# A two-layer hybrid decoder: two plain groups instead of three at the feed-forward's entry, parameters on SyncE's queue, first weights in halves, last outputs scaled by ScalarE and sent on two queues

## Chip, cores and metric

The kernel runs on one core of a Trainium2 chip. The metric is the device time of one execution in microseconds, lower is better. Times of before and after are medians of several runs; the profile shows one execution of its own.

## What is computed

Two layers on 1024 tokens of width 1024, in float32. Cut to what matters here:

```python
for l in range(DEPTH):                                   # DEPTH = 2
    h = rmsnorm(x, attn_norm[l])
    proj = h @ w_in[l]                                   # split among four mixers
    ...                                                  # attention, gated conv, pooling, windowed attention
    mixed = per_group_rmsnorm(...) * mix_norm[l]
    x = x + mixed @ w_o[l]
    h2 = rmsnorm(x, ffn_norm[l])
    gate, up = jnp.split(h2 @ w_gate_up[l], 2, axis=-1)  # D_FF = 2816 = 22 x 128
    x = x + (jax.nn.silu(gate) * up) @ w_down[l]
return rmsnorm(x, final_norm)
```

## The kernel before

**Layout.** Activations lie transposed, channels on the 128 partitions, tokens along the row in two halves of 512 (`HT`). The 1024 channels are 8 tiles (`NK`), the 2816 inner channels of the feed-forward 22 (`NFF`).

**Matmuls.** Every float32 operand is split into two parts that TensorE multiplies at its fast float32 rate: `hi`, rounded by a copy on ScalarE, and `lo`, the rest, by a subtraction on VectorE (`split`, L283 and L284; with a gain per channel L286 and L287). A product of a 128x128 block with 128x512 activations is then three matmuls (`mm3`, L272): hi by hi, hi by lo, lo by hi.

**The start.** The parameters (norm gains and such, `par`) are loaded by GpSimd's queue (L131). The weights of the first three projections and the input x (`enter`, L366) come on SyncE's queue; `weights` (L203 on) loads a tile of 128x1024 with one DMA (L207), copies it to `hi` (L215) and subtracts (L216). The x tiles are scaled with the attention norm's gains from `par` while they are split, and their squares are added up on the way (L313, L318, L324) for the norm. The list of weights to come is written by `expect_layer`.

**The feed-forward's first half** makes gate and up for 22 groups of 128 inner channels. A *plain* group (`plain`, L1268) multiplies the weight blocks with the activation blocks directly: for each half of the tokens, four products of four blocks (2 for the gate, 2 for up). The other groups pair channel tiles and token halves as 2x2 blocks and need seven products in place of eight (the loop at L1466, helper `gu_start`). They use sums of the weight blocks, made by GpSimd (`sums`, L1132 to L1134, `sum4`, L1154), and differences of the activation blocks, made by VectorE from the residual (`combine`, L1054: per pair of channel tiles the differences N1, N2, T3, T4, L1063 to L1071, each of which is then split in two). In a seven-product group the first product takes B11, the second B21 (both split when the residual is added in `out_last`, L1099), the third N2, then N1, T3, B22 and T4. Between products ScalarE copies a partial result out of PSUM (`snap`, L1176), and VectorE adds (L1188, L1512, L1524) and multiplies with the norm (`mul_to`, L348). The silu is ScalarE's (L1311), its product with the norm GpSimd's (L1312).

Three groups are plain (`NPL = 3`, L42). They are what TensorE works on while `combine`, the norm of the residual (`norm`) and the first weight sums are made; the order in which these are written is L1426 to L1465. The two half splits of a plain group's weights are `split_plain`; a seven-product group's are `split1` to `split4`, one wide split for each of the first three and a narrow one.

Beside this GpSimd adds up blocks of the down projection's weights (`dn_sums`, L161), four additions of 256 columns at a time. The activations of each pair of groups are combined on VectorE and written to DRAM (`combos`, L1314), to be read back for the down projection, which also takes seven products.

**The end.** In the last layer the last products (B22) of the down projection are made for 256 tokens at a time (L1641 on). For each piece the result is added to the residual (`evac`, L1577), squared and summed over channels, and the norm follows: a matmul with ones (L336), three steps on ScalarE (L338 to L340), two on VectorE (L341, L344). Then `finish` (L375) multiplies each of the 8 tiles by the final norm's gain and the norm in one VectorE instruction (L380) and sends it out on SyncE's queue (L384).

**The order** in which each engine works is not that of the program's text. `steps_of` lists all instructions, `length` estimates each one's duration, and `arrange` places them on the engines one after the other, by rank and by when their inputs are ready. `MOVES` shifts the rank of some 400 numbered groups of instructions by hand-set amounts (`places`), and `order_engines` fixes the resulting order for each engine. Instructions, buffers and dependencies stay what the text says.

Of the kernel before, what the change touches and what calls it, by code (L numbers as in the profile page):

```python
# [15 lines left out]
ALU = mybir.AluOpType  # L16
# [25 lines left out]
NPL = 3  # L42
# [69 lines left out]
def trunk_kernel(ctx: ExitStack, tc: tile.TileContext, ins, out):  # L112
# [18 lines left out]
    pool.dma_start(par, ins["params"])  # L131
# [71 lines left out]
    def weights(src, n):  # L203
        if n > 2 * P:
            s = F.pair()
            raw = F.ap2(s)
            sp.dma_start(raw[:, :n], src)  # L207
# [7 lines left out]
        act.copy(hi[:, :n], raw[:, :n])  # L215
        dve.tensor_tensor(out=lo[:, :n], in0=raw[:, :n], in1=rd(hi[:, :n]), op=ALU.subtract)  # L216
# [20 lines left out]
    def expect_layer(l):  # L237
        for m in (2, 3, 0, 4, 5, 6, 1, 13, 14, 10, 11, 12, None, 7, 8, 9):
            if m is None:
                expect(rope_weights, l)  # L240
            else:
                expect(weights, ins["w_in"][l, m], 2 * HT)
# [132 lines left out]
    def finish(x, t, cols):  # L375

        for d in range(NK):
            a = F.ap(x[d][t])[:, cols]
            g = par[:, L * PC_N + d : L * PC_N + d + 1]
            dve.scalar_tensor_tensor(  # L380
                out=a, in0=a, scalar=g, in1=F.ap(ratt[t])[:, cols], op0=ALU.mult, op1=ALU.mult
            )
            o = out[d, :, t * HT : (t + 1) * HT]
            sp.dma_start(o[:, cols], a)  # L384

    last_silu = None
    for l in range(L):
# [1038 lines left out]
        std.append(GateUp(2))  # L1426
# [9 lines left out]
        plain_gates()  # L1436
        combine(2)
        plain_acts()
        std[2].split_plain()
        w = GateUp(3)  # L1440
# [3 lines left out]
        w.sums()  # L1444
        combine(3)
        plain_acts()
        w.split1()
        plain(2, 0)
        plain_silus()
        plain_gates()  # L1450
        w.split2()
        plain_acts()
        wn = GateUp(4)
        plain(2, 1)
        plain_silus()
# [185 lines left out]
        for cols in (slice(0, 256), slice(256, HT)) if last else ():  # L1641
            for m, p, w in tail:
# [26 lines left out]
class Step:  # L1669
    __slots__ = ("ins", "eng", "rank", "before", "after", "tiles", "left", "ns", "tail", "ready", "sums", "bank", "onchip", "size", "start", "end", "table", "rows", "place")  # L1670

    def __init__(self, eng, rank):
# [4 lines left out]
        self.onchip = False  # L1677
# [64 lines left out]
def steps_of(tc):  # L1742
    steps, seen = [], {}
    table, runs = None, {"Silu": [], "Exp": []}
    for i in tc.nc.cur_bb.bb.instructions:
# [23 lines left out]
        elif kind == "InstDMACopy":  # L1769
# [47 lines left out]
def arrange(steps, rank=lambda v: v.rank):  # L1817
# [35 lines left out]
    while any(now.values()) or any(later.values()):  # L1853
# [57 lines left out]
        else:  # L1911
# [5 lines left out]
            if e == "DVE" and v.onchip:  # L1917
                ns += 0.8 * sum(max(0.0, min(b, t + ns) - max(a, t)) for a, b in pool_busy[-8:])
# [234 lines left out]
```

## Time and profile before

| | us |
|---|---|
| median of 3 runs | 2063.41 (2063.31 to 2064.40) |
| the profiled execution | 2062.8 |
| its span, first to last instruction | 2061.0 |
| TensorE busy | 2038.0 (99%), 9442 matmuls |
| VectorE busy | 1539.8 (75%) |
| ScalarE busy | 971.0 (47%) |
| GpSimd busy | 571.3 (28%) |
| granted TensorE clock, mean | 0.998 |

In the lines below PE is TensorE, PEld its weight loads, DVE VectorE, ACT ScalarE, POOL GpSimd, SP SyncE. A line of the timeline has the start in us, the length in us, engine, line, operation, the tiles written and read, their shapes and the count of instructions run together; in brackets the idle time ahead of it and what ended it. A line of the groups has the count, then busy us and mean ns of one, then the idle time ahead. A line of the waits has who waited for whom, the sum in us, how often, the longest. A line of a stretch has each engine's busy us and its count of instructions, the clock, the share of the DMA engines and GB/s.

### The profile page before, as it was taken

What the parts mean: (1) busy time and instruction counts of PE and PEld (TensorE: products, weight loads), DVE (VectorE), ACT (ScalarE), POOL (GpSimd) and SP (SyncE); (2) the same over time, 40 slices, a digit from 0 to 9 for tenths busy, and PEclk for the clock granted to TensorE, in tenths of its full rate; (3) what the DMA queues carried; (4) which work ended last, traced back from release to release, by engine and by line L of the source; (5) the groups of instructions that cost most, each with busy time, mean ns of one, the idle gap of its engine ahead of it and who ended that gap; (6) DMA issues with size and microseconds to landing.
All of it is one profiled execution on the core that took longest, in us unless ns stands there. A gap on an engine that the chain in (4) does not pass through costs nothing.

```text
span 2061.0 us, 26301 instructions
## 1 busy us (share of the span) xinstructions
PE 2038.0 (99%) x9442; PEld 1680.9 (82%) x9442; DVE 1539.8 (75%) x2420; ACT 971.0 (47%) x1712; POOL 571.3 (28%) x453
## 2 busy tenths in 40 slices
PE   8999999999999999999999999999999999999997
PEld 6887888887888888888888878888888888888887
DVE  7888988976766767655656898878877677786555
ACT  7547556643333334444434576656433333354332
POOL 0000000047776775100000000000677677650000
PEclk9999999999999999999999999999999999999999
DMA  5110222324444446966411102233344444498652
GB/s 181 42 45 30 74 86 98 133 103 159 168 159 152 166 158 231 340 236 208 138 36 44 57 16 86 75 118 113 133 169 158 155 163 157 143 325 303 201 177 87
DMA packets 148819, 289.76 MB, mean 141 GB/s; under 512 B 12608, under 2 KB 72000, under 8 KB 148688
## 3 DMA queue, kind: packets, MB, share of 16 engines
q1 hardware_dynamic: 148656, 288.03, 40.5%
q8 instruction: 74, 1.21, 0.2%
q14 instruction: 57, 0.47, 0.1%
q0 software_dynamic: 32, 0.04, 0.0%
HBM read 204.66 MB, written 83.36 MB: 140 GB/s over the span
## 4 chain that ended last, share of the span: by engine, by line
PE 95%; DVE 2%; ACT 1%; DMA 1%; issue 1%; POOL 0%; DVEq 0%; SPq 0%; ACTq 0%; POOLq 0%
PE ps_mm L272 36%; PE ps_s L272 29%; PE ps_t L272 12%; PE ps_pv L272 8%; PE ps_pv L962 2%; PE ps_t L950 1%; PE ps_s L896 1%; PE ps_t L336 1%; PE ps_s L897 1%; PE ps_s L898 1%; PE ps_pv L572 1%; PE ps_mm L770 1%; PE ps_s L511 1%; DVE u L284 1%; PE ps_t L560 1%
## 5 line engine op out<-in xcount | busy, mean ns | idle before, releaser
L272 PE MATMUL ps_mm<-u,u 128*128 128x512 f32 (+1 forms) x3376 | 835.5, 389 | 1.4 <-DVE u L1001 1.2
L272 PEld LDWEIGHTS ps_mm<-u,u 128*128 128x128 f32 x3376 | 621.7, 188 | 126.6 <-issue 4.0
L272 PE MATMUL ps_s<-u,u 128*128 128x512 f32 x2672 | 636.0, 390 | 9.5 <-ACT u L286 7.4
L272 PEld LDWEIGHTS ps_s<-u,u 128*128 128x128 f32 x2672 | 501.6, 188 | 116.2 <-ACT u L286 7.4
L284 DVE TENSOR_TENSOR u<-u,u 128x1024 fp32r<-128x1024 f32 (+2 forms) x380 | 449.5, 1206 | 154.1 <-ACT u L283 118.9
L283 ACT CAST u<-u 128x1024 fp32r<-128x1024 f32 (+2 forms) x380 | 328.1, 888 | 480.4 <-PE ps_mm L272 192.8
L272 PE MATMUL ps_t<-u,u 128*128 128x512 f32 (+1 forms) x1212 | 284.1, 378 | 0.0
L272 PEld LDWEIGHTS ps_t<-u,u 128*128 128x128 f32 x1212 | 222.7, 188 | 43.0 <-issue 0.5
L959 POOL MEMSET u<- 128x128 f32 x32 | 5.9, 212 | 844.8 <-PE ps_mm L272 653.0
L1312 POOL TENSOR_TENSOR tp<-tp,u 128x512 f32<-128x512 f32 x88 | 144.1, 1639 | 231.6 <-ACT tp L1311 231.3
L161 POOL TENSOR_TENSOR u<-u 128x256 f32<-128x256 f32 x176 | 188.7, 1072 | 66.4 <-DVE u L284 30.5
L272 PE MATMUL ps_pv<-u,u 128*128 128x512 f32 x696 | 167.4, 389 | 0.4 <-ACT u L283 0.4
L272 PEld LDWEIGHTS ps_pv<-u,u 128*128 128x128 f32 x696 | 130.5, 188 | 28.1 <-ACT u L283 0.8
L1311 ACT ACTIVATE tp<-tp 128x512 f32<-128x512 f32 x88 | 55.5, 632 | 127.4 <-DVE tp L348 126.7
L1132 POOL TENSOR_TENSOR u<-u,u 128x512 f32<-128x512 f32 x38 | 66.9, 1761 | 140.9 <-ACT tp L1311 83.9
L286 ACT ACTIVATE u<-u,par 128x512 fp32r<-128x512 f32 x100 | 69.9, 717 | 58.0 <-DVE u L1577 18.6
L283 ACT CAST u<-ps_t 128x512 fp32r<-128x512 f32 (+4 forms) x136 | 65.1, 506 | 56.4 <-PE ps_t L950 32.5
L284 DVE TENSOR_TENSOR u<-ps_t,u 128x512 fp32r<-128x512 f32 (+4 forms) x136 | 76.9, 582 | 18.4 <-ACT u L283 17.6
L287 DVE SCALAR_TENSOR_TENSOR u<-u,par,u 128x512 fp32r<-128x512 f32 x100 | 72.7, 745 | 7.7 <-ACT u L286 7.5
L1524 DVE TENSOR_TENSOR tp<-ps_mm,tn 128x512 f32<-128x512 f32 x38 | 26.3, 691 | 61.5 <-PE ps_mm L272 61.5
L348 DVE TENSOR_TENSOR tp<-tp,u 128x512 f32<-128x512 f32 x76 | 69.0, 908 | 1.1
L318 ACT ACTIVATE tn<-u 128x512 f32<-128x512 f32 (+1 forms) x93 | 52.8, 589 | 31.8 <-DVE u L1577 28.4
(191 smaller groups left out, 2218.9 us busy)
## 6 DMA issues: line engine op xcount, KB each, us to landing
u<-in_w_gu SPq DMA_DIRECT2D x88, 512.0 KB, 4.3
ad<-u SPq DMA_DIRECT2D x154, 256.0 KB, 2.4
u<-ad SPq DMA_DIRECT2D x70, 512.0 KB, 5.4
u<-in_w_dn SPq DMA_DIRECT2D x68, 512.0 KB, 4.0
qd<-u SPq DMA_DIRECT2D x44, 512.0 KB, 2.9
u<-qd SPq DMA_DIRECT2D x32, 512.0 KB, 4.8
u<-in_w_in SPq DMA_DIRECT2D x30, 512.0 KB, 3.5
u<-in_xT SPq DMA_DIRECT2D x32, 256.0 KB, 5.1
```

Of the source, the lines that this page charges most:

```text
L161: pool.tensor_tensor(out=o, in0=o, in1=u, op=ALU.add)
L272: pe.matmul(o, w, r, start=start and k == 0 and i == 0, stop=stop and k == n - 1 and i == 2, skip_group_check=again,)
L283: act.copy(hi, f)
L284: dve.tensor_tensor(out=lo, in0=f, in1=rd(hi), op=ALU.subtract)
L286: act.activation(hi, f, AF.Copy, scale=gain)
L287: dve.scalar_tensor_tensor(out=lo, in0=f, scalar=gain, in1=rd(hi), op0=ALU.mult, op1=ALU.subtract)
L318: act.activation(q, f, AF.Square)
L348: dve.tensor_tensor(out=o, in0=a, in1=b, op=ALU.mult)
L962: pe.matmul(py[:, c0:], v_of(j, h), R.ap(s)[:, c0:], start=j == 0 and n == 0, stop=j == nj - 1 and n == 1,)
L1132: pool.tensor_tensor(out=F.ap(q + 1), in0=a21, in1=a22, op=ALU.add)
L1311: last_silu = act.activation(g, g, AF.Silu)
L1312: pool.tensor_tensor(out=g, in0=g, in1=r, op=ALU.mult)
```

## The change

- `NPL` is 2: two plain groups, the third becomes a seven-product group. The sequence at the entry is rewritten for it; `w.sums()` and `w.split1()` of the first seven-product group come earlier in the text.
- `par` is loaded by SyncE's queue.
- The weights of the very first projection are loaded, copied and subtracted in two halves of 512 columns.
- In the last piece of the end, ScalarE multiplies each output tile by its gain (`gain`) once the tile's square is taken; `finish` then multiplies by the norm alone, and the DMAs of even tiles are issued by ScalarE, of odd ones by SyncE.
- Three of the planner's estimates are changed (a GpSimd operation, VectorE next to GpSimd, a DMA issued by ScalarE), and the table `MOVES` is replaced by another.

```diff
-NPL = 3
+NPL = 2
...
-    pool.dma_start(par, ins["params"])
+    sp.dma_start(par, ins["params"])
...
-    def weights(src, n):
+    def weights(src, n, parts=1):
+        cuts = [slice(i * n // parts, (i + 1) * n // parts) for i in range(parts)]
         if n > 2 * P:
             s = F.pair()
             raw = F.ap2(s)
-            sp.dma_start(raw[:, :n], src)
+            for c in cuts:
+                sp.dma_start(raw[:, c], src[:, c])
...
-        act.copy(hi[:, :n], raw[:, :n])
-        dve.tensor_tensor(out=lo[:, :n], in0=raw[:, :n], in1=rd(hi[:, :n]), op=ALU.subtract)
+        for c in cuts:
+            act.copy(hi[:, c], raw[:, c])
+            dve.tensor_tensor(out=lo[:, c], in0=raw[:, c], in1=rd(hi[:, c]), op=ALU.subtract)
...
-                expect(weights, ins["w_in"][l, m], 2 * HT)
+                expect(weights, ins["w_in"][l, m], 2 * HT, 2 if (l, m) == (0, 2) else 1)
...
+    def gain(x, d, t, cols):
+        a = F.ap(x[d][t])[:, cols]
+        act.activation(a, a, AF.Copy, scale=par[:, L * PC_N + d : L * PC_N + d + 1])
+
-    def finish(x, t, cols):
+    def finish(x, t, cols, gained=False):
         for d in range(NK):
             a = F.ap(x[d][t])[:, cols]
-            g = par[:, L * PC_N + d : L * PC_N + d + 1]
-            dve.scalar_tensor_tensor(
-                out=a, in0=a, scalar=g, in1=F.ap(ratt[t])[:, cols], op0=ALU.mult, op1=ALU.mult
-            )
+            if gained:
+                mul_to(a, a, F.ap(ratt[t])[:, cols])
+            else:
...
-            sp.dma_start(o[:, cols], a)
+            (act if gained and d % 2 == 0 else sp).dma_start(o[:, cols], a)
...
-        std.append(GateUp(2))
+        w = GateUp(2)
         plain(0, 0)
         combine(0)
         plain(1, 0)
...
         plain_gates()
+        w.sums()
         combine(2)
         plain_acts()
-        std[2].split_plain()
-        w = GateUp(3)
+        w.split1()
         plain(1, 1)
         plain_silus()
         plain_gates()
-        w.sums()
         combine(3)
-        plain_acts()
-        w.split1()
-        plain(2, 0)
-        plain_silus()
-        plain_gates()
         w.split2()
         plain_acts()
-        wn = GateUp(4)
-        plain(2, 1)
-        plain_silus()
-        plain_gates()
...
+        wn = GateUp(3)
         w.split3()
-        plain_acts()
         plain_silus()
...
                 evac(B22, m, p, cols)
                 ss.add(1, F.ap(x[2 * m][1])[:, cols], cols)
+                for d in (2 * m, 2 * m + 1):
+                    gain(x, d, 1, cols)
             ratt[1] = ss.rnorm(1, cols, tag="s")
-            finish(x, 1, cols)
+            finish(x, 1, cols, True)
...
-        return 206 if kind == "InstMemset" else 230 + 2.07 * n
+        return 206 if kind == "InstMemset" else 1150 + 0.5 * n
...
+            elif eng == "ACT":
+                v.ns, v.tail = 450, 2400
...
-            v.onchip = not any(a.bass_ap.tensor.name.startswith("ps_") for a in ins + outs)
+            if not any(a.bass_ap.tensor.name.startswith("ps_") for a in ins + outs):
+                v.onchip = 0.7 if kind == "InstTensorScalarPtr" and len(ins) < 3 else 0.4
...
-                ns += 0.8 * sum(max(0.0, min(b, t + ns) - max(a, t)) for a, b in pool_busy[-8:])
+                ns += v.onchip * sum(max(0.0, min(b, t + ns) - max(a, t)) for a, b in pool_busy[-8:])
```

More of the change, by code (lines that the diff above doesn't have):

```diff
@@ L373, in enter_norm @@
         ratt[t] = ss.rnorm(t, parts=True)
-    def finish(x, t, cols):
+    def gain(x, d, t, cols):
+        a = F.ap(x[d][t])[:, cols]
+        act.activation(a, a, AF.Copy, scale=par[:, L * PC_N + d : L * PC_N + d + 1])
+    def finish(x, t, cols, gained=False):
         for d in range(NK):
             a = F.ap(x[d][t])[:, cols]
-            g = par[:, L * PC_N + d : L * PC_N + d + 1]
-            dve.scalar_tensor_tensor(
-                out=a, in0=a, scalar=g, in1=F.ap(ratt[t])[:, cols], op0=ALU.mult, op1=ALU.mult
-            )
+            if gained:
+                mul_to(a, a, F.ap(ratt[t])[:, cols])
+            else:
+                g = par[:, L * PC_N + d : L * PC_N + d + 1]
+                dve.scalar_tensor_tensor(
+                    out=a, in0=a, scalar=g, in1=F.ap(ratt[t])[:, cols], op0=ALU.mult, op1=ALU.mult
+                )
             o = out[d, :, t * HT : (t + 1) * HT]
-            sp.dma_start(o[:, cols], a)
+            (act if gained and d % 2 == 0 else sp).dma_start(o[:, cols], a)
     last_silu = None
@@ L1676, in __init__ @@
         self.sums = self.bank = None
-        self.onchip = False
+        self.onchip = 0.0
         self.table = self.rows = None
```

93 rows, old and new, of the table MOVES are left out of this document.

## The prediction

> **What bounds the kernel now.** I read the page's busy shares first, then what TensorE waited for, then single stretches of the timeline.
>
> ```profile
> PE 2038.0 (99%) x9442; PEld 1680.9 (82%) x9442; DVE 1539.8 (75%) x2420; ACT 971.0 (47%) x1712; POOL 571.3 (28%) x453
> PE   8999999999999999999999999999999999999997
> ```
>
> ```profile
> PE ps_s L272 <- ACT u L286: 7.4, 1, 7.4
> PE ps_s L336 <- DVE u L320: 1.4, 1, 1.4
> PE ps_mm L272 <- DVE u L1001: 1.2, 1, 1.2
> PE ps_s L272 <- DVE te L1512: 1.0, 1, 1.0
> PE ps_s L272 <- DVE tp L348: 0.5, 1, 0.5
> PE ps_s L272 <- ACT tn L1176: 0.5, 1, 0.5
> PE ps_pv L272 <- ACT u L283: 0.4, 1, 0.4
> ```
>
> TensorE works in 38 of 40 slices at nine tenths or more. What it waits for is 7.4 us ahead of its first matmul and, in these rows, 5.0 us in all behind it; L1512, L348, L1176 and the 0.4 us of L283 lie in the feed-forward's entry of layer 0 and make 2.4 us. So a microsecond of matmul work taken out is a microsecond of time, as long as nobody else is late; and little waiting is left for a better order to remove. A matmul's recorded 390 ns overlaps its neighbour, so its price comes from start to start:
>
> ```profile
> 1464.21 5.60 PE L272 MATMUL ps_s<-u,u 128*128 128x512 f32 x24
> 1469.65 5.60 PE L272 MATMUL ps_t<-u,u 128*128 128x512 f32 x24
> 1475.09 2.88 PE L272 MATMUL ps_s<-u,u 128*128 128x512 f32 x12
> ```
>
> Two runs of 24 start 5.44 us apart: 0.2267 us a matmul.
>
> **The change part by part. 1, a plain group less.** A product is 4 blocks by 3 matmuls, 12 in all. A plain group makes 4 products for each half of the tokens, 96 matmuls; a group by seven products makes 84. Each layer turns one plain group into a seven-product one: 12 matmuls fewer, 24 over both layers, 24 x 0.2267 = **-5.4 us**. The 22 groups load the same weights and write the same activations, so DMA in this stage does not change. Beside TensorE it adds work. On ScalarE there are three copies out of PSUM and one half-width split more, which I cost at nothing: ScalarE is a third busy (24.29 of 72 us in the row for 460 to 532 below). GpSimd gets four sums more per layer. VectorE loses two wide splits and four products of 512 columns and gets three wide splits, a narrow one and seven operations of 512 columns.
>
> **2, the entry.** That work meets a shorter cover. In both layers the plain products start when the last residual is added, and the first product that needs a difference (N2) comes behind all plain products and two seven-group products. In layer 1 that is 1410 to 1480.5, in layer 0 393 to 460:
>
> ```profile
> core 0: us, PE busy (x) PEld busy (x) DVE busy (x) ACT busy (x) POOL busy (x), PEclk, DMA share, GB/s
> 1410.00:1480.50 70.50, 70.50 (x312) 58.33 (x311) 61.57 (x80) 34.86 (x55) 21.67 (x14) 1.00 0.28 97
> ...
> 393.00:460.00 67.00, 66.53 (x294) 54.55 (x293) 52.81 (x73) 33.06 (x52) 18.71 (x12) 1.00 0.24 83
> 460.00:532.00 72.00, 70.05 (x305) 56.24 (x304) 52.54 (x52) 24.29 (x34) 50.56 (x39) 1.00 0.50 172
> ```
>
> ```profile
> L284 DVE TENSOR_TENSOR u<-tp,u 128x512 fp32r<-128x512 f32 x16 | 10.7, 682 | 0.5 <-ACT u L283 0.4
> L284 DVE TENSOR_TENSOR u<-u,u 128x1024 fp32r<-128x1024 f32 x7 | 10.1, 1445 | 3.2 <-PE ps_mm L272 3.1
> ```
>
> The deadline comes 96 x 0.2267 = 21.8 us sooner, so layer 1's window shrinks to 48.7 us. VectorE's 61.6 us in it lose the plain group's two wide splits and four products, 2 x 1.445 + 4 x 0.68 = 5.6 us: 56.0 us for 48.7, 7.3 too many. What may be put off is 12 of the 16 splits of differences (only N2's four are due): 12 x 0.68 = 8.2 us. So it fits, with 0.9 us to spare, if the written order puts them off and they are back before N1, T3 and T4 are due, at steps of 2.7 us. Layer 0 has 52.8 - 5.6 = 47.2 us for 67 - 21.8 = 45.2, 2.0 too many, and again something to put off. The bounds: the present 2.4 us of waits all gone, or 7.3 + 2.0 = 9.3 us of new waiting and more where GpSimd is in the way (below). Since the work fits if sorted, I choose a value near the small end: **+1.0 us**.
>
> **3, the start.** First matmul, x tile and parameters:
>
> ```profile
> 0.75 0.38 SPq L207 DMA_DIRECT2D u<-in_w_in  x1
> 1.18 0.90 SPq L366 DMA_DIRECT2D u<-in_xT  x2
> 1.26 0.70 POOL L131 DMA_DIRECT2D par<-in_params  x1 [0.81 <-POOLq L2139]
> ...
> 5.60 0.63 ACT L313 ACTIVATE u<-u 128x512 f32<-128x512 f32 x1 [0.18 <-DMA u<-in_xT]
> 6.66 1.33 ACT L286 ACTIVATE u<-u,par 128x512 fp32r<-128x512 f32 x2 [0.42 <-DMA par<-in_params]
> 7.43 3.29 PE L272 MATMUL ps_s<-u,u 128*128 128x512 f32 x6 [7.43 <-ACT u L286]
> ```
>
> ```profile
> 4.00:6.50 2.50, 0.00 (x0) 0.00 (x0) 1.05 (x1) 1.67 (x2) 0.00 (x0) 1.00 0.87 220
> 6.50:9.00 2.50, 1.57 (x3) 0.97 (x4) 1.92 (x5) 2.34 (x4) 0.00 (x0) 1.00 1.03 400
> ```
>
> ```profile
> 7.43:27.00 19.57, 19.57 (x78) 15.70 (x79) 19.51 (x31) 17.65 (x29) 0.00 (x0) 1.00 0.87 330
> ```
>
> The first x tile is there at 5.60, but its scaling (L286) waits for the parameters until 6.66. On SyncE's queue they cost one issue of about 0.4 us ahead of the weights, the second half another, and they come first. If only the parameters are early, the scaling runs at 5.60 in place of the square, and TensorE starts 0.77 us behind it, at 6.4: 1.0 us gained. If the low rate of 4 to 6.5 us (220 against 400 GB/s) goes with GpSimd's transfer too, some 2.5 x (400 - 220) / 400 = 1.1 us of transfer comes forward: 2.0 us. The low end is nothing: from the first matmul to 27 us VectorE is busy 19.51 of 19.57 us, and TensorE cannot run ahead of it for long. Halving adds a second cast and subtraction, some 0.2 us each, ahead of the first x tile at most. The waits removed lie on the path, so I stand between: **-1.4 us**. The next late thing is the second x tile, then VectorE.
>
> ```profile
> 8.81 1.91 PE L272 MATMUL ps_s<-u,u 128*128 128x512 f32 x4
> 10.52 0.80 PE L272 MATMUL ps_mm<-u,u 128*128 128x512 f32 x2
> ```
>
> Four of the first matmuls start 1.71 us ahead of the next, 0.43 us each and not 0.23: the start is slow for a while whatever feeds it. [...]
>
> **4, the end.**
>
> ```profile
> 2049.64 0.42 DVE L1577 TENSOR_TENSOR u<-u,ps_mm 128x256 f32<-128x256 f32 x1 [2.59 <-PE ps_mm L272]
> ...
> 2054.12 3.26 DVE L380 SCALAR_TENSOR_TENSOR u<-u,par,u 128x256 f32<-128x256 f32 x8
> ```
>
> ```profile
> L384 SPq DMA_DIRECT2D out<-u x24: 332/388/408, 2026.6 to 2058.0; - x24
> ```
>
> ```profile
> 2054.63 3.75 SPq L384 DMA_DIRECT2D out<-u  x8
> ```
>
> ```profile
> L380 DVE SCALAR_TENSOR_TENSOR u<-u,par,u 128x256 f32<-128x256 f32 x16 | 6.5, 479 | 0.1
> L324 DVE TENSOR_TENSOR u<-u,tn 128x256 f32<-128x256 f32 x3 | 1.3, 422 | 0.1
> L318 ACT ACTIVATE tn<-u 128x256 f32<-128x256 f32 x4 | 1.7, 413 | 8.1 <-DVE u L1577 8.1
> ```
>
> Eight products take 3.26 us, 0.40 apart ((3.26 - 0.48) / 7); eight issues take 3.75 us, 0.48 apart, the last at 2058.0. The queue sets the end. With four issues a queue, each has 0.8 us for a 0.4 us issue, and the products set it: without the scalar they cost 422 in place of 479 ns, 0.34 apart, so the eighth ends at 2054.12 + 7 x 0.34 + 0.42 = 2056.9 and is issued 0.1 us later, 1.0 us ahead of now. Without any gain per product it would be 2057.4, 0.6 us ahead. ScalarE's 16 scalings (some 0.45 us each) lie under the last matmuls; the last two fit where ScalarE waits 1.3 us ahead of L338. If that cover were gone, 0.9 us would be added. No row shows an issue by ScalarE: SyncE's take 0.4 us and GpSimd's 0.70, and I take SyncE's, since both have the time. Bounds 0 and 1.1, taken **-0.9 us**.
>
> **5, the new order.** The table of moves is replaced and three cost figures with it; they add no instruction. Outside start, entry and end the rows of waits hold 1.2 us (L1001), so there is little to win and something to lose. Taken 0.
>
> Sum: -5.4 + 1.0 - 1.4 - 0.9 = **-6.7 us**. The profiled execution took 2062.8 us for a span of 2061.0 (1.8 around it) and would take 2056.1; the median is 0.6 above it, so I give 2063.4 - 6.7 = **2056.7 us**.
>
> **The rivals.** *The entry gives most of it back.* VectorE's excess is put off only in part: half of 7.3 in layer 1 and the 2.0 of layer 0, 5.7 us. For it speaks that VectorE worked 61.6 of 70.5 us there; against it, that layer 1 has no wait at all in its entry now. 2063.4 - 5.4 - 2.3 + 5.7 = 2061.4.
>
> *GpSimd's added sums hold VectorE, and the change is slower.* The same split of a difference, 682 ns in layer 1's entry, takes 993 in layer 0's, where GpSimd works:
>
> ```profile
> L284 DVE TENSOR_TENSOR u<-tp,u 128x512 fp32r<-128x512 f32 x7 | 6.7, 993 | 0.0
> L1071 DVE SCALAR_TENSOR_TENSOR tp<-u,nffn,tp 128x512 f32<-128x512 f32 x8 | 5.9, 742 | 0.0
> L1050 DVE SCALAR_TENSOR_TENSOR u<-u,u 128x512 f32<-128x512 f32 x44 | 51.8, 1178 | 0.7
> L1132 POOL TENSOR_TENSOR u<-u,u 128x512 f32<-128x512 f32 x38 | 66.9, 1761 | 140.9 <-ACT tp L1311 83.9 <-PE ps_s L272 38.3 <-PE ps_pv L272 10.8
> ```
>
> An operation of 742 ns is 1178 in the stage full of GpSimd sums. If nothing is put off (9.3 us) and each of the eight added sums delays VectorE by those 0.44 us while TensorE waits (3.5), 12.8 us stand against 7.7: 2068.5. It decides from 11.8 us of new waiting on (0.2% above now). Against it: the sums can run while GpSimd is idle, 49 of the 70.5 us. [...]
>
> *The new order also removes the old waits*: no added 1.0, the entry's 2.4 and L1001's 1.2 gone, 2056.7 - 4.6 = 2052.1.
>
> *Start and end bring nothing* (VectorE full, scaled outputs no sooner): 2056.7 + 2.3 = 2059.0; I count it with the forecast.
>
> **How the numbers follow.** Forecast 0.64 (its own range 2053 to 2059.2), entry gives back 0.15, slower 0.07, old waits gone too 0.14. A measurement of this kernel tells about 0.2%, 4.1 us, from no change: below 2059.3 is faster (0.64 + 0.14 = 0.78), up to 2067.5 the same (0.15), above it slower (0.07). The range, 2051 to 2062, leaves out the slower rival, the upper third of the first rival and the lower third of the last.
>
> **What would show it.** Right: 24 records of 128x512 fewer on TensorE; a first matmul between 5.4 and 6.4 us; eight last outputs issued from two engines, the last at about 2.9 us behind the first product; under 3.5 us of waits between first N2 product and the fourth seven-product group. Wrong: waits of TensorE in layer 1's entry for VectorE's splits or for GpSimd's sums of more than 3 us, a scaling of ScalarE ahead of the last L338, or new waits of over 2 us in the mixers, which no step here prices.

## The result and the profile after

The changed kernel takes 2069.72 us (median of 12 runs, 2067.51 to 2072.89), the kernel before 2064.18 us in the same session (12 runs, 2062.72 to 2067.30). The ratio is 1.0027, with a 95% interval of 1.0019 to 1.0035: some 5.5 us slower, where 6.7 us faster was forecast. The profiled execution took 2068.78 us for a span of 2067.0, against a span of 2061.0 before.

First the busy times, then TensorE's longest waits in the changed kernel. Its lines are numbered anew: L275 was L272, L287 was L284, L289 was L286; L390 and L351 are the products in `finish` with and without the gain.

```profile
PE 2036.0 (99%) x9418; PEld 1676.0 (81%) x9418; DVE 1549.2 (75%) x2431; ACT 987.8 (48%) x1739; POOL 592.5 (29%) x460
```

```profile
PE ps_mm L275 <- ACT u L289: 9.2, 1, 9.2
PE ps_mm L275 <- DVE u L1577: 1.9, 1, 1.9
PE ps_s L275 <- DVE te L1512: 1.9, 2, 1.5
PE ps_s L275 <- ACT tn L1186: 1.5, 2, 1.2
PE ps_s L339 <- DVE u L323: 1.4, 1, 1.4
PE ps_pv L275 <- DVE te L1512: 1.4, 1, 1.4
PE ps_mm L275 <- DVE u L287: 1.3, 1, 1.3
```

The 24 matmuls are gone (9418 for 9442), so the work did shrink. But TensorE now starts at 9.2 us instead of 7.4, waits 1.9 us near the end for a residual sum (L1577), and 6 us in these rows for VectorE and for copies out of PSUM (L1512, L1186, L287), in the two entries.

The entries show best in two stretches of 160 us, one per layer. The count behind TensorE's busy time is what matters: 160 us hold 706 matmuls at 0.2267 us. First before, then after.

```profile
400.00:560.00 160.00, 157.59 (x689) 128.19 (x688) 118.80 (x133) 62.26 (x91) 91.05 (x67) 1.00 0.39 135
1400.00:1560.00 160.00, 160.00 (x707) 132.25 (x706) 130.80 (x152) 71.97 (x110) 80.73 (x58) 1.00 0.38 135
```

```profile
400.00:560.00 160.00, 156.08 (x684) 127.50 (x683) 126.85 (x145) 67.67 (x101) 99.37 (x70) 1.00 0.41 145
1400.00:1560.00 160.00, 157.00 (x686) 127.82 (x685) 138.41 (x159) 77.68 (x117) 86.53 (x62) 1.00 0.41 143
```

In layer 1, 21 matmuls fewer were made in the same time: 21 x 0.2267 = 4.8 us. To say where time went, I take each matmul's start and subtract the steady work ahead of it (0.2267 us for 512 columns, 0.1733 for 384, 0.1200 for 256, 0.057 for 128, the spacing of undisturbed stretches in both traces). What this lag grows by in a stretch is **lost** there.

| us | before | after | difference |
|---|---|---|---|
| steady matmul work | 1985.8 | 1980.3 | -5.4 |
| lag of the first matmul | 7.4 | 9.2 | +1.8 |
| lost from there to 400 us (layer 0's mixers) | 26.5 | 27.9 | +1.4 |
| lost 400 to 560 (entry of layer 0) | 4.3 | 5.4 | +1.1 |
| lost 1050 to 1400 (layer 1's mixers) | 24.8 | 25.7 | +0.9 |
| lost 1400 to 1560 (entry of layer 1) | 0.2 | 4.8 | +4.6 |
| lost from 2000 us to the last matmul | 2.4 | 4.6 | +2.2 |
| from the last matmul's start to the end of the span | 9.7 | 8.9 | -0.7 |

The column of differences adds up to 5.9 of the 6.0 us by which the spans differ. In the timelines below, rows that do not bear on the point are left out. The start, the timeline after:

```profile
1.64 0.42 SPq L131 DMA_DIRECT2D par<-in_params  x1
2.11 2.80 SPq L369 DMA_DIRECT2D u<-in_xT  x6
7.24 1.95 ACT L289 ACTIVATE u<-u,par 128x512 fp32r<-128x512 f32 x3 [2.46 <-DMA u<-in_xT]
9.23 0.80 PE L275 MATMUL ps_mm<-u,u 128*128 128x512 f32 x1 [9.23 <-ACT u L289]
```

The parameters are early, but the x tiles come behind them and in another order: the new table loads and scales tiles 2 and 3 first, and the first product needs tile 0, which is the third of the three scalings. It ends at 9.19 us, the first matmul starts at 9.23. The stretch of low transfer stayed, too, with no transfer of GpSimd in it:

```profile
4.00:6.50 2.50, 0.00 (x0) 0.00 (x0) 1.75 (x6) 0.72 (x2) 0.00 (x0) 1.00 0.77 197
```

The tail, the timeline after, where the whole tiles of the first half are finished:

```profile
2029.78 4.72 PE L275 MATMUL ps_mm<-u,u 128*128 128x256 f32 x38
2030.32 5.38 DVE L390 SCALAR_TENSOR_TENSOR u<-u,par,u 128x512 f32<-128x512 f32 x8
2035.95 0.42 DVE L1577 TENSOR_TENSOR u<-u,ps_mm 128x256 f32<-128x256 f32 x1
2036.42 7.58 PE L275 MATMUL ps_mm<-u,u 128*128 128x256 f32 x61 [1.93 <-DVE u L1577]
```

Of TensorE's 38 matmuls, the first 33 are a product for the first 256 tokens (11 blocks of three). The next one to use that PSUM tile, for the other 256, waits until L1577 has read it, and L1577 stands behind eight instructions of `finish`. The end itself, the same view:

```profile
2060.79 2.77 DVE L351 TENSOR_TENSOR u<-u,u 128x256 f32<-128x256 f32 x8
2062.26 1.86 ACTq L394 DMA_DIRECT2D out<-u  x4
```

The eight products are 0.34 us apart ((2.77 - 0.42) / 7), four of the issues are ScalarE's, and the last starts at 2063.70, 2.91 us behind the first product: as forecast.

### The profile page after: what moved, and what is told of

It is laid out like the page before. It is cut to its first block, busy times and chain, and to the rows that moved or that the text cites. A ratio compares the mean times of both kernels' runs of the same rounds, so it can differ in the third digit from the quotient of the medians.

```text
span 2067.0 us, 26301 instructions
## 1 busy us (share of the span) xinstructions
PE 2036.0 (99%) x9418; PEld 1676.0 (81%) x9418; DVE 1549.2 (75%) x2431; ACT 987.8 (48%) x1739; POOL 592.5 (29%) x460
## 4 chain that ended last, share of the span: by engine, by line
PE 89%; DVE 5%; ACT 2%; DMA 2%; POOL 1%; issue 1%; SPq 0%; DVEq 0%; ACTq 0%; POOLq 0%
PE ps_mm L275 35%; PE ps_s L275 26%; PE ps_t L275 10%; PE ps_pv L275 7%; PE ps_pv L972 2%; PE ps_t L960 1%; DVE u L287 1%; PE ps_s L906 1%; PE ps_t L339 1%; PE ps_s L907 1%; PE ps_s L908 1%; PE ps_pv L582 1%; PE ps_s L521 1%; PE ps_mm L780 1%; ACT u L286 1%
## 5 line engine op out<-in xcount | busy, mean ns | idle before, releaser
L275 PE MATMUL ps_mm<-u,u 128*128 128x512 f32 (+1 forms) x3394 | 850.6, 390 | 13.8 <-ACT u L289 9.2
L275 PEld LDWEIGHTS ps_mm<-u,u 128*128 128x128 f32 x3394 | 622.0, 189 | 141.5 <-ACT u L289 9.4
L275 PE MATMUL ps_s<-u,u 128*128 128x512 f32 x2648 | 644.4, 389 | 3.4 <-DVE te L1512 1.9
L275 PEld LDWEIGHTS ps_s<-u,u 128*128 128x128 f32 x2648 | 496.3, 188 | 109.1 <-ACT tn L1186 3.1
L287 DVE TENSOR_TENSOR u<-u,u 128x1024 fp32r<-128x1024 f32 (+2 forms) x384 | 461.2, 1223 | 151.7 <-ACT u L286 128.5
L286 ACT CAST u<-u 128x1024 fp32r<-128x1024 f32 (+2 forms) x384 | 332.0, 888 | 452.8 <-PE ps_mm L275 174.5
L275 PE MATMUL ps_t<-u,u 128*128 128x512 f32 (+1 forms) x1146 | 270.0, 378 | 0.9 <-DVE u L1109 0.4
L275 PEld LDWEIGHTS ps_t<-u,u 128*128 128x128 f32 x1146 | 206.3, 188 | 42.5 <-DVE u L1109 1.3
L161 POOL TENSOR_TENSOR u<-u 128x256 f32<-128x256 f32 x176 | 197.6, 1123 | 75.6 <-DMA u<-in_w_dn 40.0
L1322 POOL TENSOR_TENSOR tp<-tp,u 128x512 f32<-128x512 f32 x88 | 146.5, 1666 | 238.8 <-ACT tp L1321 235.5
L275 PE MATMUL ps_pv<-u,u 128*128 128x512 f32 x744 | 181.3, 389 | 1.4 <-DVE te L1512 1.4
L275 PEld LDWEIGHTS ps_pv<-u,u 128*128 128x128 f32 x744 | 139.6, 188 | 30.8 <-DVE te L1512 1.8
L286 ACT CAST u<-ps_t 128x512 fp32r<-128x512 f32 (+4 forms) x136 | 64.6, 506 | 66.8 <-PE ps_t L570 25.4
L289 ACT ACTIVATE u<-u,par 128x512 fp32r<-128x512 f32 x100 | 69.9, 717 | 52.0 <-DVE u L1577 18.0
L287 DVE TENSOR_TENSOR u<-ps_t,u 128x512 fp32r<-128x512 f32 (+4 forms) x136 | 76.5, 583 | 20.5 <-ACT u L286 17.7
L351 DVE TENSOR_TENSOR tp<-tp,u 128x512 f32<-128x512 f32 x80 | 73.2, 914 | 1.1
L219 DVE TENSOR_TENSOR u<-u,u 128x1024 fp32r<-128x1024 f32 (+2 forms) x47 | 51.9, 1108 | 26.4 <-PE ps_t L275 11.5
```

The source lines that it names most:

```text
L161: pool.tensor_tensor(out=o, in0=o, in1=u, op=ALU.add)
L219: dve.tensor_tensor(out=lo[:, c], in0=raw[:, c], in1=rd(hi[:, c]), op=ALU.subtract)
L275: pe.matmul(o, w, r, start=start and k == 0 and i == 0, stop=stop and k == n - 1 and i == 2, skip_group_check=again,)
L286: act.copy(hi, f)
L287: dve.tensor_tensor(out=lo, in0=f, in1=rd(hi), op=ALU.subtract)
L289: act.activation(hi, f, AF.Copy, scale=gain)
```

## Experiments

Theories: **A**, the edits are worth what was forecast, but the newly written order loses it, in start, tail and entries; **B**, two plain groups cover too little, whatever the order; **C**, GpSimd's sums take VectorE's time in the entry, which is then short; **D**, against C, VectorE is short without GpSimd, too. Later **E**: the planner that writes the order does not know what a meeting of the two engines costs; and **F**: the change's new estimates spoiled an order that the old ones would have written well.

**e1_start.** The start's edits alone, on the kernel before; its moves, with the parameters' load sent to the front.

```diff
-    pool.dma_start(par, ins["params"])
+    sp.dma_start(par, ins["params"])
...
+                expect(weights, ins["w_in"][l, m], 2 * HT, 2 if (l, m) == (0, 2) else 1)
...
 MOVES = {
+    0: -178,
```

> The kernel before with the start's two edits alone (parameters on SyncE's queue, first weights in two halves), and the table of moves of before, in which only the parameters' load is moved to the front. Theory A (the start is late because the new order loads and scales x tiles 2 and 3 ahead of tile 0, for which TensorE's first product waits): here x tile 0 comes first, the first matmul is at 6.3 to 7.4 us (before 7.43, after 9.23), and the time is between 1.1 us less and the same as before. Theory B (the two edits themselves delay the x tiles, by three issues of about 0.4 us ahead of them and small packets): first matmul at 8.4 us or later, time 1 to 2 us above before.

2064.13 us, ratio to before 1.0004 (0.9994 to 1.0014). The timeline:

```profile
1.65 0.90 SPq L369 DMA_DIRECT2D u<-in_xT  x2
4.92 1.04 ACT L218 CAST u<-u 128x1024 fp32r<-128x1024 f32 x1 [2.90 <-DMA u<-in_w_in]
6.17 0.72 ACT L289 ACTIVATE u<-u,par 128x512 fp32r<-128x512 f32 x1 [0.21 <-DMA u<-in_xT]
6.95 0.79 PE L275 MATMUL ps_s<-u,u 128*128 128x512 f32 x1 [6.95 <-ACT u L289]
```

With tile 0 first, the scaling starts as soon as the tile is there, as the forecast had it. A holds. But nothing is gained: in the three other runs with the start as before (e2, e3, e10) the first matmul came at 6.7 to 6.8 us, so 7.4 was one execution's value, and at 400 us the lag was 34.2 against 34.0 before. The halves are not tried on the first product here: its weights come whole (L218, 1024 columns at 4.92 us), because the moves of before put another projection's first. In the changed kernel the halved ones come first.

**e7_new_order_old_start.** The counter-test: the changed kernel with the start's two edits undone, its own moves kept (in which group 11, x tiles 2 and 3, is sent further ahead than group 6, tiles 0 and 1).

```diff
-    sp.dma_start(par, ins["params"])
+    pool.dma_start(par, ins["params"])
...
 MOVES = {
     6: -160, 11: -188,
```

> The changed kernel with its table of moves, but the start as before: parameters on GpSimd's queue, first weights in one piece. Theory A (the table sends x tiles 2 and 3 first and scales them first, and TensorE's first product needs tile 0): first matmul at 8.5 us or later as in the changed kernel (9.23). Theory B (the two edits of the start delay it): first matmul at 7.5 us or sooner.

2070.78 us in one run. The timeline:

```profile
5.86 1.50 ACT L286 ACTIVATE u<-u,par 128x512 fp32r<-128x512 f32 x2
7.74 0.72 ACT L286 ACTIVATE u<-u,par 128x512 fp32r<-128x512 f32 x1 [0.38 <-DMA u<-in_xT]
8.51 0.79 PE L272 MATMUL ps_mm<-u,u 128*128 128x512 f32 x1 [8.51 <-ACT u L286]
```

Two tiles are scaled and TensorE still waits for the third. At 8.51 us this just meets A's bound; the order makes at least 1.1 us of the delay, and the edits at most the 0.7 us up to 9.2.

**e2_tail.** The end's edits alone, with the moves of before.

```diff
+                for d in (2 * m, 2 * m + 1):
+                    gain(x, d, 1, cols)
...
-            finish(x, 1, cols)
+            finish(x, 1, cols, True)
```

> The kernel before with the edits of the end alone (ScalarE multiplies by the gain, last outputs on two queues), with the moves of before. Theory A (the 2 us that TensorE waits near 2034 us come from the new order, which puts the first half's eight products of finish ahead of a residual sum that TensorE needs): no wait of TensorE over 0.5 us in the last 40 us, some 0.7 us less from the last matmul to the end, time 0.5 to 0.9 us below before. Theory B (the wait belongs to the edit, whose scalings fill ScalarE): a wait of 1.5 us or more for the residual sum appears here too, time 1 us or more above before.

2063.00 us, ratio 0.9995 (0.9986 to 1.0004): a gain too small for the measurement. Its profile shows it: 8.9 us from the last matmul's start to the end instead of 9.7, no wait in the tail but the norm's, 2.4 us lost there as before. A holds: the profiled execution gives the edit 0.8 us at the end, and the new wait is the order's.

**e3_entry.** Two plain groups alone, the planner's estimates and moves of before.

```diff
-NPL = 3
+NPL = 2
...
-        std.append(GateUp(2))
+        w = GateUp(2)
```

> The kernel before with two plain groups and the entry's new text alone; the planner's estimates are those of before, its moves too, carried over to the same groups of instructions where these exist. TensorE has 5.4 us less to do. Theory A (the entry is lost by the order that the new table writes): this other order loses less than 2 us more than before in each entry, and the time is 2 us or more below before. Theory B (VectorE and GpSimd have too much to do for two plain groups' cover, whatever the order): 4 us or more of new waiting in layer 1's entry again, time within 2 us of before or above it.

2080.83 us, ratio 1.0083 (1.0068 to 1.0099): 16.8 us slower with 5.4 us less work. 14.9 us were lost in layer 0's entry and 9.3 in layer 1's. By its letter that is B's outcome, but it is far beyond the changed kernel's 5.4 and 4.8 with the same work, so the order alone can move the entries by 14 us. It tells that order matters, not that a good one exists.

**e4_short_sums.** The changed kernel's order to the instruction, with GpSimd's weight sums cut from 512 to 16 columns. The rest of each sum is left out, and the third wide split takes raw weights in place of a sum.

```diff
-                pool.tensor_tensor(out=F.ap(q), in0=a21, in1=a11, op=ALU.add)
+                pool.tensor_tensor(out=F.ap(q)[:, c], in0=a21[:, c], in1=a11[:, c], op=ALU.add)
...
-                self.sq = pair_split(self.q)
+                self.sq = pair_split(self.raw[1])
```

> The changed kernel with its written order kept instruction by instruction, but GpSimd's four weight sums of each seven-product group work on 16 columns in place of 512, and the third wide split reads the raw weights; the products that use those sums are thus left wrong. Theory C (GpSimd's sums stretch VectorE's instructions, and this fills the entry): the waits in layer 1's entry, 1400 to 1560 us, fall from 4.9 us to under 1.5, in layer 0's, 400 to 560, from 5.4 to under 3. Theory D (VectorE has too much to do, or in the wrong order, with GpSimd idle too): over 3.5 us stay in layer 1's entry.

2061.21 us in one run, 8.5 below the changed kernel. The two stretches:

```profile
400.00:560.00 160.00, 158.75 (x698) 130.10 (x697) 112.62 (x147) 69.45 (x103) 58.04 (x73) 1.00 0.44 149
1400.00:1560.00 160.00, 159.57 (x702) 131.16 (x701) 122.82 (x157) 76.58 (x114) 53.36 (x64) 1.00 0.41 140
```

2.3 and 1.2 us lost. VectorE made as many instructions as in the changed kernel (147 for 145, 157 for 159) in 14 and 16 us less. D falls: without the sums the same order loses little. VectorE's instructions are longer beside GpSimd's, as C has it. Two things are not shown by it: that there is then too little VectorE for the work, and that the longer instructions alone make the loss. The splits that need a sum get it sooner here, too; in the changed kernel ScalarE's casts for such splits (L286) wait 8.8 and 5.8 us for sums in layer 0's entry.

**e5_mixed_order.** All edits, with the moves of before for the start, the mixers and the last products, and those of the changed kernel for both feed-forwards.

```diff
 MOVES = {
-    0: -178, 3: -184, 6: -160, 11: -188, 16: -162, 21: -153, 26: 87, 27: -184,
+    0: -178, 3: -96, 6: -115, 11: -89, 16: -86, 27: -169,
...
-    4633: -132, 4634: 66, 4644: 172, 4646: 169, 4649: -101,
+    4625: -97, 4629: -25, 4633: -52, 4634: -114, 4646: -346, 4648: -51, 4649: -139,
```

> The changed kernel with all its edits; the table of moves is that of before (carried over to the same groups of instructions) up to the first layer's entry, in the second layer's mixers and in the last products, and that of the changed kernel in both feed-forwards. Theory A (start, mixers and tail lose by the new table, the entries by something else): first matmul by 7.4 us, no wait over 0.5 us at 2030 to 2040 us, the entries as in the changed kernel (5.4 and 4.9 us lost); time 2064 us, 5 to 6 us below the changed kernel and no different from before. Rival (edits, not order, cost the time outside the entries): start, mixers and tail lose 5 us as in the changed kernel, time 2069.

2065.30 us, ratio 1.0009 (1.0000 to 1.0018): 4.4 us below the changed kernel, one less than expected. First matmul at 6.9 us, 2.4 us lost in the tail, with no wait at 2030 to 2040 us: for the first matmul and the tail A holds. The entries lose 3.9 and 3.9, less than the 5.4 and 4.9 expected. The start's gain is gone by 400 us: 2.5 us go at 350 to 400 (1.1 in the changed kernel), and the lag there is 37.3 us against the changed kernel's 37.1. So this run does not price the start.

**e6_late_down_sums.** The same, with GpSimd's additions for the down projection's weights held back.

```diff
-            if not end:
+            if not end and f > NPL + 1:
                 next(sums, None)
...
-            if n < 5:
+            if n < 6:
```

> The run above, but GpSimd's additions for the down projection's weights (12 of 256 columns for each two groups) start two seven-product groups later, and one more is done at the start of the down projection; moves as above for all other groups. Theory C (GpSimd's work stretches VectorE's and this holds the entry): less GpSimd work there, the entries lose 2 to 5 us less, time 2059 to 2062. Theory D (the order, or VectorE's own work, holds the entry): within 1 us of the run above.

2066.64 us, ratio 1.0013 (1.0005 to 1.0022), 6.0 and 3.7 us lost in the entries. GpSimd worked less (87 for 97 us in 400 to 560), and nothing was won: the 2 to 5 us that C expected did not come. This does not refute C's mechanism, for the order is another one: with GpSimd's instructions gone, the planner placed others elsewhere, and a single wait of 2.3 us came up, which with the slow matmuls behind it (last section) makes 3.9 of layer 0's 6.0. It suggests that not the sum of the meetings counts, but whether the order reckons with them.

How a meeting looks can be read in the changed kernel's own trace. VectorE and GpSimd, 437 to 447 us:

```profile
437.54 1.22 DVE L287 TENSOR_TENSOR u<-u,u 128x1024 fp32r<-128x1024 f32 x1
438.68 0.68 DVE L1060 SCALAR_TENSOR_TENSOR tp<-tp,te 128x512 f32<-128x512 f32 x1
439.28 0.69 DVE L287 TENSOR_TENSOR u<-tp,u 128x512 fp32r<-128x512 f32 x1
440.26 1.40 DVE L287 TENSOR_TENSOR u<-tp,u 128x512 fp32r<-128x512 f32 x1 [0.30 <-ACT u L286]
441.58 1.77 DVE L1079 TENSOR_TENSOR tp<-te 128x512 f32<-128x512 f32 x1
...
446.29 0.68 DVE L351 TENSOR_TENSOR u<-ps_mm,tp 128x512 f32<-128x512 f32 x1
446.89 0.68 DVE L1198 TENSOR_TENSOR tp<-ps_t,tn 128x512 f32<-128x512 f32 x1
```

```profile
437.79 3.32 POOL L1322 TENSOR_TENSOR tp<-tp,u 128x512 f32<-128x512 f32 x1 [8.66 <-ACT tp L1321]
441.07 1.73 POOL L1164 TENSOR_TENSOR u<-u 128x512 f32<-128x512 f32 x1
446.44 1.30 POOL L1142 TENSOR_TENSOR u<-u,u 128x512 f32<-128x512 f32 x1 [3.63 <-DVE tp L1081]
```

L1322 ends at 441.11, the VectorE instruction begun at 440.26 ends 0.55 us behind it; GpSimd's next ends at 442.80, VectorE's next 0.55 us behind that. They run one after the other, and the record of each holds its wait: 0.68 becomes 1.77 for VectorE, 1.30 becomes 3.32 for GpSimd. The two that read PSUM (446.29 and 446.89) keep their 0.68 beside a sum that keeps its 1.30. The planner takes a fixed share of the common time instead, 0.8 before and 0.4 or 0.7 after the change. So E: let it reckon with the exclusion.

**e11_lock_price_alone.** The changed kernel with the planner alone altered: the two kinds of operation exclude each other in it, a GpSimd sum of 512 columns has 1.29 us, and a matmul waits for the reader of the other half of its PSUM tile.

```diff
+def locks(e, v):
+    aps = [a for a in v.ins[0].ins if hasattr(a, "bass_ap")]
+    if any(a.bass_ap.tensor.name.startswith("ps_") for a in aps):
+        return False
+    if e == "POOL":
+        return type(v.ins[0]).__name__ == "InstTensorTensor"
+    return e == "DVE" and sum(width(a) > 64 for a in aps) > 1
...
-            if e == "DVE" and v.onchip:
-                ns += v.onchip * sum(max(0.0, min(b, t + ns) - max(a, t)) for a, b in pool_busy[-8:])
+            both = locks(e, v)
+            if both and held[1] != e:
+                ns += max(0.0, held[0] - t)
...
+            if both:
+                held = v.end - (80 if e == "DVE" else 100), e
...
-        return 206 if kind == "InstMemset" else 1150 + 0.5 * n
+        return 206 if kind == "InstMemset" else 60 + 2.4 * n
...
-                cross = name.startswith("ps_") and w == writes
+                cross = name.startswith("ps_")
```

> The changed kernel, its whole table of moves and all its edits, with nothing altered but the planner: the two engines' SBUF operations exclude each other, and a matmul into one half of a PSUM tile waits for the reader of the other half. Theory E (the price of the meeting decides in the entries, the rest is start and tail): entries under 2 us each, first matmul still at 8.5 to 9.3 us, time 2056 to 2061, 9 to 13 us below the changed kernel. Rival (the gain of the two runs before came from the moves of start and tail, taken from before): time 2064 or more.

2058.64 us, ratio 0.9975 (0.9965 to 0.9985). Its longest waits and its two stretches:

```profile
PE ps_mm L275 <- ACT u L289: 9.2, 1, 9.2
PE ps_s L339 <- DVE u L323: 1.4, 1, 1.4
PE ps_mm L275 <- ACT u L218: 1.0, 1, 1.0
PE ps_mm L275 <- DVE u L287: 0.6, 1, 0.6
```

```profile
400.00:560.00 160.00, 159.40 (x700) 130.65 (x699) 130.44 (x148) 71.46 (x106) 105.72 (x74) 1.00 0.45 151
1400.00:1560.00 160.00, 159.80 (x702) 130.92 (x701) 137.37 (x155) 77.87 (x117) 92.47 (x64) 1.00 0.41 140
```

11.1 us below the changed kernel's median, with the same edits and the same table. 1.6 and 1.2 us lost in the entries, 2.4 in the tail; the first matmul is still at 9.2. VectorE and GpSimd are busier in layer 0's entry than in the changed kernel (130.4 for 126.9, 105.7 for 99.4): they still meet, but TensorE waits less for it. E's forecast holds, and B falls. E's cause is the exclusion only if the other two changes to the planner do not matter; that is taken up below.

**e8_lock_order.** The same planner, with start and tail moves of before.

```diff
 MOVES = {
-    0: -178, 3: -184, 6: -160, 11: -188, 16: -162, 21: -153, 26: 87, 27: -184,
+    0: -178, 3: -96, 6: -115, 11: -89, 16: -86, 27: -169,
```

> The changed kernel with all its edits and its table of moves (that of before for the first 50 groups, the start, and for the last products), but the planner, when it writes the order, lets an operation of VectorE with two inputs in SBUF and a sum of GpSimd run only one after the other, as the traces show it (a VectorE operation of 0.68 us that meets one of GpSimd's takes up to 1.78, one that reads PSUM stays at 0.68). No instruction is added. Theory E (the entries lose because the order was written with too cheap a meeting of the two engines; with the right price the work fits): the entries lose under 2 us each in place of 5.4 and 4.9, time 2055 to 2060. Theory B (two plain groups cover too little, whatever the order): 4 us or more stay in each entry, time 2063 or more.

2055.79 us, ratio 0.9961 (0.9948 to 0.9975). First matmul at 6.6 us, 1.5 and 0.4 us lost in the entries, 2.4 in the tail. Against e11 only the moves of start and tail differ, and both lose 2.4 us in the tail: the start's order is worth the 2.9 us between their medians (2.0 us show in the lag at 400 us, 33.8 for 35.8; the intervals of the two ratios overlap). The two stretches:

```profile
400.00:560.00 160.00, 159.38 (x701) 130.70 (x700) 130.28 (x145) 70.08 (x103) 108.20 (x74) 1.00 0.44 147
1400.00:1560.00 160.00, 160.00 (x706) 131.79 (x705) 134.04 (x153) 75.70 (x114) 93.75 (x66) 1.00 0.41 138
```

**e9_lock_order_refit** and **e10_three_plain_refit.** The same planner with moves fitted anew, once with two plain groups and all edits, once with three and the end's edits. (The fitting left 490 and 555 of the moves other than they were, not some 30 as the expectation says.) The kernel with three has the start of before, too.

```diff
-NPL = 2
+NPL = 3
```

> As the run above, with some 30 moves around TensorE's waits fitted anew for this planner. Theory E: entries under 2 us each, time 2052 to 2058. Theory B: 4 us or more in each entry, time 2062 or more.

> The kernel before with three plain groups and the edits of the end, under the same planner and with moves fitted anew in the same way. If the seven-product group is worth its 5.4 us once the order is right (theory E), this run stands 4.5 to 6.5 us above the run before it, at about 2059 to 2062. If two plain groups cover too little whatever the order (theory B), it stands no more than 2 us above, or below it.

2055.70 us, ratio 0.9960 (0.9947 to 0.9974), with two; 2060.94 us, ratio 0.9987 (0.9978 to 0.9996), with three. They stand 5.2 us apart by their medians, and both lose under 1 us in each entry: under an order that fits, the difference agrees with the 5.4 us of the group. The two traces are only 2.1 us apart: the profiled execution with three, 2057.94 us, is the fastest of its 11, and from 1050 to 1400 us it loses 23.6 us, against 26.8 with two. So the 5.2 is known to a microsecond or two at best. The refit adds nothing to e8.

**e12_old_estimates.** The moves of e8, in a planner without the exclusion and the half tile, and with two of the change's three estimates as they were before it. The third, a DMA issued by ScalarE, stays as the change has it.

```diff
-        return 206 if kind == "InstMemset" else 1150 + 0.5 * n
+        return 206 if kind == "InstMemset" else 230 + 2.07 * n
...
-                v.onchip = 0.7 if kind == "InstTensorScalarPtr" and len(ins) < 3 else 0.4
+                v.onchip = 0.8
```

> The changed kernel with start and tail moves of before, its own moves for the rest, and the planner's three estimates of before (a meeting of the engines at 0.8 of the time that they share, a GpSimd sum of 512 at 1.29 us). Theory F (the change's cheaper estimates, 0.4 to 0.7, spoiled an order that the old ones would have written well): entries lose under 3 us each, time 2056 to 2060. Theory E (neither estimate has the exclusion, and the old ones write no better order): 4 us or more in each entry, time 2062 to 2068.

2067.82 us, ratio 1.0021 (1.0011 to 1.0030), 7.0 and 6.9 us lost in the entries:

```profile
400.00:560.00 160.00, 155.35 (x677) 125.85 (x676) 124.59 (x142) 65.04 (x98) 97.93 (x71) 1.00 0.42 143
1400.00:1560.00 160.00, 156.40 (x677) 127.37 (x677) 132.30 (x157) 76.43 (x116) 84.73 (x61) 0.99 0.41 141
```

F falls: with this table the change's new estimates are no worse than the old, and neither fixed share writes an order that fits. That none could, with a table fitted to it, is not shown; the kernel before, with 0.8 and three plain groups, loses 4.3 and 0.2.

## Why the prediction was wrong

**1, the work: right.** -5.4 us, shown by the count of matmuls, and e9 against e10 (5.2 by the medians) agrees.

**2, the entry: the step that failed most.** It was priced +1.0 "since the work fits if sorted". The work does fit: with e11's order the entries lose 1.7 us less than before ((1.6 - 4.3) + (1.2 - 0.2)), close to the better end of the bounds (-2.4). But the order in the kernel was taken to be sorted, and it is not: +1.1 in layer 0 and +4.6 in layer 1, together 5.7. The forecast had read the stretched instructions beside GpSimd from the rows (682 and 993 ns) without asking whether the planner that writes the order knows them, though its estimates stood in the diff. It had also listed what VectorE gains and counted only what it loses; VectorE is busy 8.1 and 7.6 us more in the two stretches. That alone is not the failure, for in e11 it is 11.6 and 6.6 us more and little is lost. In layer 1 the longest wait is the 1.4 us ahead of 1513.7 us, where TensorE needs L1512 and VectorE has three wide splits ahead of it. The last of them takes 2.32 us beside a GpSimd instruction, where the other two take 1.22:

```profile
1508.49 4.59 DVE L287 TENSOR_TENSOR u<-u,u 128x1024 fp32r<-128x1024 f32 x3 [0.74 <-DMA ad<-u]
1513.01 0.68 DVE L1512 TENSOR_TENSOR te<-ps_pv,tn 128x512 f32<-128x512 f32 x1
```

**3, the start: sign wrong.** -1.4 forecast; +1.8 at the first matmul and +3.2 by 400 us in these two executions, +2.9 by the medians of e11 and e8. With the start's order of before the lag at 400 us is 34 to 36 us (e1, e2, e3 and e10 beside the kernel before), so a single trace prices the start to some 2 us. The step assumed that the tile order stays and that only the parameters come earlier. The new table put x tiles 2 and 3 first (e7). And the 7.4 us of the trace were taken for a fixed wait: with the start unchanged it is 6.7 to 7.4, and the parameters on the other queue left no measurable gain (e1); in no run did the first matmul come before 6.6 us, where 5.4 to 6.4 was the sign of being right. Its better bound of -2.0 rested on GpSimd's transfer slowing the rest; the low rate is there without it (197 GB/s).

**4, the end: right,** -0.7 for -0.9, by the mechanism described. What it missed is upstream: the same tail lost 2.2 us more by the order of `finish` and L1577 (e2, e5, e8, e11: gone).

**5, the new order: priced 0, and the cause of the rest.** "They add no instruction" is true and not enough. With another planner (e11) the same edits and the same table of moves take 11.1 us less. By the table above, start and tail are 5.4 of the loss (3.2 and 2.2), the entries 5.7, layer 1's mixers 0.9: 12.0 in all, against 6.1 gained by less work and the end. Why the mixers lose differently from run to run of these kernels (25.9 us in e8 and 26.8 in e9 from 1050 to 1400, 24.8 before) was not tried.

**The rivals.** *The entry gives most of it back* had the entry's size (+5.7), but by luck: it took VectorE's own excess for the cause, and with the sums cut (e4) the same VectorE instructions leave little loss. It had nothing of start and tail. *GpSimd's added sums hold VectorE* came closest in time (2068.5) by another sum: 12.8 us in the entries, where 5.7 were lost. That the two engines stretch each other's instructions is seen: in the rows at 437 to 443 us they run one after the other, and 0.68 us becomes 1.77. But such instructions cost TensorE little where the order expects them: e11 loses 1.6 and 1.2 us in the entries, with both engines busier than in the changed kernel in layer 0's (130.4 for 126.9, 105.7 for 99.4). *The new order also removes old waits* needed an order that fits, and e8 and e9 have one; at 2055.8 and 2055.7 us they are nearer to the forecast's 2056.7 than to its 2052.1. That they meet the forecast's number is luck in part: their entries lose 2.6 and 3.0 us less than before where 1.0 more was forecast, and the start gives nothing where 1.4 was.

What stays open: e11 changes three things in the planner at once (the exclusion, the length of a sum, the half PSUM tile). The length is not it: e12 has the same 1.29 us and loses 7 us in each entry. The half tile fits the tail's wait for L1577. In the two stretches of the entries it has nothing to act on: all their matmuls and all instructions that read PSUM take 512 columns, in the changed kernel and in e11. So the exclusion is left. Chance is an unlikely rival: with two plain groups, the three orders written with the exclusion lose 1.5 to 2.8 us in both entries together, the six written without it (e4, with its sums cut, apart) 7.8 to 24.2. No run adds the exclusion alone, and how VectorE's longer instructions and the sums' later ends share the loss is not told apart.

## What to carry to other kernels

When a schedule is written by a planner, a change of its table or estimates is an edit with a price of its own: look for pairs of engines whose records stretch when they meet, and ask whether the planner has that in its form, here an exclusion, and not only in its factor. A count "it fits if sorted" bounds the gain; it does not say that the order at hand is sorted. And before a new structure is given up, run it under an order that suits it: here the same edits stood at 2069.7 and at 2055.8 us.

## What the runs showed of the hardware

By the recorded starts GpSimd does not always get the next turn when it waits for one: its instruction recorded from 437.79 us met a VectorE split begun at 437.54, and two VectorE instructions that started later, back to back with that one (438.68 and 439.28), still went ahead of it, 3.32 us in all; it got in where VectorE had a gap of 0.30 us. It is the longest of GpSimd's instructions in the traces of the two kernels; the next takes 2.36 us. Whether a recorded start is the moment at which GpSimd asks for its turn, the trace does not show.

A wait of 2.3 us was followed by half of TensorE's rate. In e6, the timeline and the granted clock (the last but two of the columns):

```profile
458.57 1.59 PE L275 MATMUL ps_s<-u,u 128*128 128x512 f32 x5 [2.28 <-DVE te L1512]
459.96 0.63 PE L275 MATMUL ps_t<-u,u 128*128 128x512 f32 x1
460.39 0.63 PE L275 MATMUL ps_s<-u,u 128*128 128x512 f32 x1
```

```profile
459.00:463.00 4.00, 4.00 (x13) 3.09 (x12) 4.00 (x4) 2.03 (x3) 3.92 (x3) 0.58 0.00 0
```

The matmuls stand 0.43 us apart until 462.95, at a clock of 0.58. Some eight of them cost 0.2 us more each, 1.6 us on top of the wait: a wait in such an entry can be dearer than it is long. This wait is not alone: in e3 a wait of 2.09 us ahead of 1487.17 us was followed by a clock of 0.57, and in e12 two waits of 1.13 and 1.41 us within 3 us (ahead of 1511.66 and 1514.49) by matmuls 0.43 us apart; the mean clock of 1400 to 1560 us is 0.99 in both. Single waits of 1.92 us (e3, ahead of 1399.16) and 1.93 us (the changed kernel, ahead of 2036.42) were followed by the full rate (0.12 us for each 256 columns in the changed kernel).
